# Four Strassen row pairs instead of three in the second MLP product of a fp32 encoder trunk

## The chip, the cores and the metric

The kernel runs on one core of a Trainium2 chip. The metric is the device time of one execution in microseconds. TensorE (PE) multiplies, ScalarE (ACT) and VectorE (DVE) prepare operands and take results out of PSUM, GpSimd (POOL) and SyncE (SP) issue transfers.

## The reference, cut to what matters

Two layers of an encoder with 256 tokens, a model width of 2048 and an MLP width of 8192, all in float32:

```python
for l in range(DEPTH):                       # DEPTH = 2
    ...                                      # attention, gates, x = x + merged @ w_out[l]
    h = rmsnorm(x, norm_mlp[l]) @ w_ff1[l]                 # 256x2048 @ 2048x8192
    x = x + jnp.square(jax.nn.relu(h)) @ w_ff2[l]          # 256x8192 @ 8192x2048
return rmsnorm(x, norm_final)
```

The second product, `@ w_ff2[l]`, is the one that the change touches.

## The kernel before

**Products in three passes.** Each float32 operand is split into `hi`, a cast to fp32r on ACT, and `lo`, the remainder, a subtraction on DVE. A product of two blocks is then three matmuls: hi·hi, lo·hi and hi·lo, all of them L428 in `mm` inside `gemm_s` (L415 to L486). The split of weights is in `parts` (L173): L177 is the cast on ACT that writes a `hi` tile, L178 the subtraction on DVE that writes a `lo` tile and needs that `hi`.

**Row pairs.** `gemm_s` makes 256x1024 of output from 2048 rows of weights, in eight *row pairs* of 2x128 rows, which I number 0 to 7. One transfer from SP brings a pair (`raw`, 128x2048, 1 MB). A pair is done in one of two ways:

- *plain*: eight block products, 24 matmuls of 128x512, accumulating into four PSUM banks. ACT casts and DVE subtracts 2048 columns of weights.
- *Strassen*: seven products, 21 matmuls, into seven banks. For them DVE first forms four sums of weight blocks, in the tile `sums`: L465 (1024 columns), L468 and L469 (512 each). Then the three raw blocks that are used themselves (1536 columns) and the four sums (2048 columns) each go through L177 and L178. The same sums are needed of the activations, once for each pair; `sums_of` (L359, four small operations L364 to L367) makes them when the pair is transposed in `turned_pair` (L391), which also splits them (ACT L407, DVE L408).

Inside a pair (`products`, L430) all matmuls that read `hi` tiles of weights come first, then those that read `lo`.

**Buffers.** In the MLP half there are three `hi` buffers and three `lo` buffers of 2048 columns (L175), three `raw` buffers, one `sums` buffer (L460), 52 slots for activations and eight PSUM banks, one name for all of them (`bank`). A Strassen pair uses two of the three `hi` buffers and two of the three `lo` buffers.

**Loops.** The MLP goes in four blocks of 2048 hidden columns. In each block `gemm_s` runs twice on `w_ff1` (Strassen pairs 3 and 5, table `FIRST`), then twice on `w_ff2` (table `SECOND`); in the last block the second of these is replaced by plain products (`gemm_a`). I call the two products on `w_ff2` in a block *the first half* (output columns 0 to 1023) and *the second half* (1024 to 2047). That makes seven of them in a layer and 14 in all: eight first halves and six second halves. The hidden pairs 4 to 7 are transposed while the first half runs.

**End of a product.** The eight banks are combined into four results: one copy on ACT (L477, from the bank of product 1, which only Strassen pairs use, so that it is complete after the last of them), then eight additions on DVE (L476). The next product gets its banks from there.

**Order.** Each engine's instructions stand in one fixed order. It is made when the program is built, by a scheduler with its own model of durations; at run time an engine waits at an instruction whose operands or buffers are not ready, and everything behind it on that engine waits too.

```python
FIRST, SECOND = (3, 5), (2, 4, 6)                                       # L65
hi, lo = (wpool.tile([P, 2048 if strips else 1024], F32R, tag=tag, name=tag,
                     bufs=3 if strips else hbufs)[:, :src.shape[-1]] for tag in ("hi", "lo"))
w11, w22, w21 = cut(raw[:, 512:])                                       # L470
w1, w3, w2, w4 = cut(whole_ts) if strips else cut(ts[0]) + cut(ts[1])   # L471
```

## Time and profile before

| | us |
|---|---|
| median of 3 runs | 2631.06 (2629.96 to 2631.34) |
| the profiled execution | 2630.92 |
| its span, first to last instruction | 2629.1 |
| PE busy | 2599.1 (99%) |
| DVE busy | 2116.7 (81%) |
| ACT busy | 1457.8 (55%) |
| DMA, mean rate | 194 GB/s |

Busy time is the union of an engine's instructions. A matmul of 512 columns is shown with 390 ns, but matmuls are pipelined: what one costs is read from the distance between starts. A row of the timeline merges neighbours of one kind: start, duration, engine, line, operation, output and inputs, form, count, and in brackets the idle time of the engine before it with what ended it.

### The profile page before, as it was taken

The page shows a single profiled execution, that of the slowest core. Times are in us where ns is not written, and L with a number is a line of the kernel's source. Part 1 is how long each engine was busy: PE and PEld are TensorE (multiplying, and loading weights), DVE is VectorE, ACT ScalarE, POOL GpSimd, SP SyncE. Part 2 cuts the span into 40 slices and gives each one's busy share as a digit, 9 for nine tenths or more (in the row PEclk, how much of TensorE's full clock was granted, in tenths as well). Part 3 has the DMA queues.
Part 4 walks back from the last instruction along what each step waited for, and adds up shares of the span by engine and source line. Part 5 has one row for each costly group of instructions (what it writes and reads, how often), then busy time and mean ns, then how long its engine had stood idle before and what let it go on. Part 6 is the DMA issues. An engine that isn't in the chain of part 4 may idle for free.

```text
span 2629.1 us, 32272 instructions
## 1 busy us (share of the span) xinstructions
PE 2599.1 (99%) x12498; PEld 2183.3 (83%) x12498; DVE 2116.7 (81%) x2496; ACT 1457.8 (55%) x1719; POOL 97.2 (4%) x117
## 2 busy tenths in 40 slices
PE   8999999999999999999999999999999999999998
PEld 7888888878888888888888888888788888888886
DVE  6678789789888888888667787896998888888885
ACT  6555556546655545546545555564566555455553
POOL 1100000000000010000001000000000000100000
PEclk9999999999999999999999999999999999999999
DMA  7555555555567485675565555644555765756744
GB/s 243 182 159 192 192 195 170 162 179 192 200 198 242 160 244 199 199 241 178 190 195 174 173 180 190 207 146 160 188 196 192 217 210 195 244 196 198 259 160 148
DMA packets 175258, 508.97 MB, mean 194 GB/s; under 512 B 13696, under 2 KB 18176, under 8 KB 175104
## 3 DMA queue, kind: packets, MB, share of 16 engines
q1 hardware_dynamic: 166192, 490.08, 55.7%
q0 software_dynamic: 8768, 16.78, 3.3%
q8 instruction: 98, 1.61, 0.2%
q14 instruction: 56, 0.46, 0.1%
q10 hardware_dynamic: 144, 0.04, 0.0%
HBM read 492.18 MB, written 2.10 MB: 188 GB/s over the span
## 4 chain that ended last, share of the span: by engine, by line
PE 76%; issue 19%; DVE 2%; ACT 1%; POOL 1%; DMA 0%; SPq 0%; POOLq 0%; DVEq 0%; ACTq 0%
PE bank L428 47%; PE bank L244 8%; PE bank L279 7%; PE bank L248 4%; PE bank L283 3%; PE bank L223 1%; PE bank L398 1%; DVE lo L178 1%; PE bank L252 1%; PE bank L224 1%; PE bank L254 1%; PE bank L253 1%; POOL xt L870 1%; PE bank L558 0%; ACT hi L177 0%
## 5 line engine op out<-in xcount | busy, mean ns | idle before, releaser
L428 PE MATMUL bank<-hi,pair 128*128 128x512 f32 x5156 | 1269.8, 390 | 7.0 <-ACT hi L177 6.2
L428 PEld LDWEIGHTS bank<-hi,pair 128*128 128x128 f32 x5156 | 964.9, 188 | 210.6 <-ACT hi L177 9.9
L177 ACT CAST hi<-raw 128x2048 fp32r<-128x2048 f32 (+3 forms) x416 | 630.0, 1534 | 449.1 <-PE bank L428 323.0
L178 DVE TENSOR_TENSOR lo<-raw,hi 128x2048 fp32r<-128x2048 f32 (+3 forms) x416 | 751.0, 1817 | 94.7 <-ACT hi L177 61.5
L428 PE MATMUL bank<-lo,pair 128*128 128x512 f32 x2578 | 677.4, 389 | 0.0
L428 PEld LDWEIGHTS bank<-lo,pair 128*128 128x128 f32 x2578 | 483.7, 188 | 100.2
L178 DVE TENSOR_TENSOR lo<-sums,hi 128x2048 fp32r<-128x2048 f32 (+1 forms) x134 | 254.6, 1909 | 176.3 <-ACT hi L177 118.5
L177 ACT CAST hi<-sums 128x2048 fp32r<-128x2048 f32 (+1 forms) x134 | 214.8, 1603 | 290.3 <-DVE sums L469 187.4
L202 DVE TENSOR_TENSOR lo<-raw,hi 128x1024 fp32r<-128x1024 f32 (+1 forms) x224 | 268.7, 1205 | 121.9 <-ACT hi L201 114.2
L201 ACT CAST hi<-raw 128x1024 fp32r<-128x1024 f32 (+1 forms) x224 | 230.0, 1036 | 208.6 <-PE bank L279 84.8
L244 PE MATMUL bank<-hi,pair 128*128 128x512 f32 x1024 | 259.6, 390 | 0.0
L244 PEld LDWEIGHTS bank<-hi,pair 128*128 128x128 f32 x1024 | 190.6, 188 | 38.9
L476 DVE TENSOR_TENSOR wide<-wide,bank 128x512 f32<-128x512 f32 x336 | 216.1, 680 | 4.5 <-PE bank L428 4.1
L279 PE MATMUL bank<-pair,hi 128*128 128x512 f32 x768 | 203.2, 397 | 4.5 <-ACT hi L201 3.2
L279 PEld LDWEIGHTS bank<-pair,hi 128*128 128x128 f32 x768 | 136.3, 190 | 26.9 <-ACT hi L201 3.6
L248 PE MATMUL bank<-lo,pair 128*128 128x512 f32 x512 | 142.8, 392 | 0.0
L465 DVE TENSOR_TENSOR sums<-raw 128x1024 f32<-128x1024 f32 x110 | 134.1, 1219 | 5.7 <-DMA raw<-in_w_ff 5.1
L283 PEld LDWEIGHTS bank<-pair,lo 128*128 128x128 f32 x768 | 106.9, 190 | 8.7
L283 PE MATMUL bank<-pair,lo 128*128 128x256 f32 x768 | 111.6, 283 | 0.0
L248 PEld LDWEIGHTS bank<-lo,pair 128*128 128x128 f32 x512 | 95.2, 188 | 18.9
L408 DVE TENSOR_TENSOR pair<-wide,pair 128x512 fp32r<-128x512 f32 x108 | 72.4, 686 | 13.9 <-ACT pair L407 13.9
L870 POOL DMA_DIRECT2D xt<-wide x48 | 42.3, 968 | 977.0 <-DVE wide L476 702.6
(131 smaller groups left out, 1727.8 us busy)
## 6 DMA issues: line engine op xcount, KB each, us to landing
raw<-in_w_ff SPq DMA_DIRECT2D x256, 1024.0 KB, 5.2
raw<-in_w_in SPq DMA_DIRECT2D x124, 1024.0 KB, 5.1
raw<-in_w_out SPq DMA_DIRECT2D x32, 1024.0 KB, 5.3
raw<-in_w_o_na SPq DMA_DIRECT2D x16, 1024.0 KB, 5.0
raw<-in_w_o_mla SPq DMA_DIRECT2D x16, 1024.0 KB, 5.0
xt<-wide POOLq DMA_DIRECT2D x48, 256.0 KB, 6.8
raw<-in_w_ukv SPq DMA_DIRECT2D x8, 1024.0 KB, 5.6
raw<-in_w_uq SPq DMA_DIRECT2D x8, 768.0 KB, 4.6
```

The lines of the kernel that those rows point to most:

```text
L177: nc.scalar.copy(hi, src)
L178: nc.vector.tensor_tensor(lo, src, hi.bitcast(F32), op=ALU.subtract)
L201: nc.scalar.copy(hi, src)
L202: nc.vector.tensor_tensor(lo, src, hi.bitcast(F32), op=ALU.subtract)
L244: nc.tensor.matmul(ps[t], a, wh[:, k], start=k0 + k + i == 0, stop=False)
L248: nc.tensor.matmul(ps[t], sides(have(acts, k0 + k), t)[0], wl[:, k], start=False, stop=k0 + k == nk - 1)
L279: nc.tensor.matmul(ps[m], wh[:, k, m * P:(m + 1) * P], have(acts, k0 + k), start=k0 + k == 0, stop=False)
L283: nc.tensor.matmul(ps[m][:, :S], wl[:, k, m * P:(m + 1) * P], have(acts, k0 + k)[:, :S], start=False, stop=k0 + k == nk - 1)
L408: nc.vector.tensor_tensor(lw, src, h.bitcast(F32), op=ALU.subtract)
L428: nc.tensor.matmul(b[i], x, y, start=count[i] == 1, stop=count[i] == total[i])
L465: nc.vector.tensor_tensor(ts[0].rearrange("p (a n) -> p a n", a=2), raw[:, :512].rearrange("p (a n) -> p a n", a=1).to_broadcast([P, 2, 512]),
L476: add = lambda o, a, c: nc.vector.tensor_tensor(o, a, c, op=ALU.add)
```

## The change

One table entry: the pairs that go by Strassen's algorithm in the second MLP product.

```diff
-FIRST, SECOND = (3, 5), (2, 4, 6)
+FIRST, SECOND = (3, 5), (2, 3, 5, 6)
```

In each of the 14 products on `w_ff2`, pairs 0, 1, 4 and 7 are plain now and 2, 3, 5 and 6 are Strassen. Before, a plain pair stood between any two Strassen pairs; now 2 and 3 are neighbours, and 5 and 6. Each of the eight blocks also has one more hidden pair whose sums are formed. SP's and POOL's orders are the same as before; on PE, DVE and ACT the scheduler makes another order.

**DVE, second half of a block.** Before, from the last weight sum of one Strassen pair (L469) to that of the next:

```order
L469 TENSOR_TENSOR sums<-raw,sums 128x512
L178 TENSOR_TENSOR lo<-sums,hi 128x2048
L178 TENSOR_TENSOR lo<-raw,hi 128x2048
L465 TENSOR_TENSOR sums<-raw 128x1024
L178 TENSOR_TENSOR lo<-raw,hi 128x1536
L468 TENSOR_TENSOR sums<-raw,sums 128x512
L469 TENSOR_TENSOR sums<-raw,sums 128x512
```

Now, from pair 2 to pair 3 (the first six rows) and on to pair 5:

```order
L469 TENSOR_TENSOR sums<-raw,sums 128x512
L178 TENSOR_TENSOR lo<-sums,hi 128x2048
L178 TENSOR_TENSOR lo<-raw,hi 128x1536
L465 TENSOR_TENSOR sums<-raw 128x1024
L468 TENSOR_TENSOR sums<-raw,sums 128x512
L469 TENSOR_TENSOR sums<-raw,sums 128x512
L178 TENSOR_TENSOR lo<-sums,hi 128x2048
L178 TENSOR_TENSOR lo<-raw,hi 128x2048
L465 TENSOR_TENSOR sums<-raw 128x1024
L178 TENSOR_TENSOR lo<-raw,hi 128x1536
L468 TENSOR_TENSOR sums<-raw,sums 128x512
L469 TENSOR_TENSOR sums<-raw,sums 128x512
```

Between neighbours the plain pair's subtraction (2048 columns from `raw`) is gone, and the three sums stand directly behind one another; from 3 to 5 the order is the old one. From 5 to 6 it is as from 2 to 3.

**PE, second half of a block**, from the first matmul on the sums of a Strassen pair. Before, one period (the `hi x20` rows are eight matmuls on the sums and twelve of the plain pair behind):

```order
L428 MATMUL bank<-hi,pair 128x512 x20
L428 MATMUL bank<-lo,pair 128x512 x4
L428 MATMUL bank<-hi,pair 128x512 x6
L428 MATMUL bank<-lo,pair 128x512 x8
L428 MATMUL bank<-hi,pair 128x512 x4
L428 MATMUL bank<-lo,pair 128x512 x3
L428 MATMUL bank<-hi,pair 128x512 x20
```

Now, from pair 2's sums to pair 6's (a `hi x14` row is eight on the sums of pair 2 or 5 and six on the raw blocks of pair 3 or 6; the `hi x20` rows begin with the sums of pair 3 and of pair 6):

```order
L428 MATMUL bank<-hi,pair 128x512 x14
L428 MATMUL bank<-lo,pair 128x512 x7
L428 MATMUL bank<-hi,pair 128x512 x20
L428 MATMUL bank<-lo,pair 128x512 x4
L428 MATMUL bank<-hi,pair 128x512 x6
L428 MATMUL bank<-lo,pair 128x512 x8
L428 MATMUL bank<-hi,pair 128x512 x4
L428 MATMUL bank<-lo,pair 128x512 x3
L428 MATMUL bank<-hi,pair 128x512 x14
L428 MATMUL bank<-lo,pair 128x512 x7
L428 MATMUL bank<-hi,pair 128x512 x20
```

From one Strassen pair's sums to the next there were 20+4+6+8+4+3 = 45 matmuls; now there are 14+7 = 21 between neighbours and 45 between pairs 3 and 5.

**ACT, first half of a block**, now, from the cast of pair 5's sums:

```order
L177 CAST hi<-sums 128x2048
L177 CAST hi<-raw 128x1536
L477 COPY wide<-bank 128x512
L177 CAST hi<-sums 128x2048
L177 CAST hi<-raw 128x2048 x3
```

The copy L477 that begins the end of the product now stands ahead of the cast of pair 6's sums, in all 14 products; before, it stood behind the casts of pair 7 and of the next product's pair 0.

In the first half, one product on the sums of pair 2 and one on those of pair 3 (two `hi` matmuls and one `lo` each) are also put off: on PE the matmuls of pair 4 end with `lo x8`, then come

```order
L428 MATMUL bank<-hi,pair 128x512 x8
L428 MATMUL bank<-lo,pair 128x512
L428 MATMUL bank<-hi,pair 128x512 x2
L428 MATMUL bank<-lo,pair 128x512 x4
L428 MATMUL bank<-hi,pair 128x512 x14
```

that is six on pair 5's raw blocks, then two and one on the sums of pair 2, two and one on those of pair 3, three on pair 5, and only then pair 5's sums (the first eight of `hi x14`). Until these are done, two of the three `hi` buffers are held by the sums of pairs 2 and 3.

## The prediction

> **What bounds the kernel now.** I read the waits of PE first, then the stages by window.

> ```profile
> PE 2599.1 (99%) x12498; PEld 2183.3 (83%) x12498; DVE 2116.7 (81%) x2496; ACT 1457.8 (55%) x1719; POOL 97.2 (4%) x117
> PE bank L428 <- ACT hi L177: 6.2, 6, 1.1
> core 0: us, PE busy (x) PEld busy (x) DVE busy (x) ACT busy (x) POOL busy (x), PEclk, DMA share, GB/s
> 924.10:1094.90 170.80, 170.80 (x772) 141.91 (x771) 141.56 (x128) 92.81 (x75) 7.06 (x8) 1.00 0.66 209
> 924.10:965.40 41.30, 41.30 (x184) 34.20 (x183) 34.96 (x29) 19.60 (x14) 3.52 (x4) 1.00 0.76 230
> 1046.80:1094.90 48.10, 48.10 (x222) 40.09 (x221) 40.55 (x43) 28.20 (x28) 0.00 (x0) 1.00 0.57 192
> ```

> PE is the bound. Its L428 matmuls waited for ACT's casts 6.2 us in all, six times, and never over 1.1 us. In one MLP block (170.8 us) it is never idle, while DVE is busy 141.6. Shares hide the rest, though: in the second half of a block (about 924 to 965) DVE is busy 35.0 of 41.3, and in the first half (about 1047 to 1095) 40.6 of 48.1. So I look at how DVE gets through the second half (start, duration; [idle before]):

> ```profile
> 937.57 0.68 DVE L469 TENSOR_TENSOR sums<-raw,sums 128x512 f32<-128x512 f32 x1
> 940.31 2.29 DVE L178 TENSOR_TENSOR lo<-sums,hi 128x2048 fp32r<-128x2048 f32 x1 [2.05 <-ACT hi L177]
> 942.72 2.29 DVE L178 TENSOR_TENSOR lo<-raw,hi 128x2048 fp32r<-128x2048 f32 x1
> 944.93 1.22 DVE L465 TENSOR_TENSOR sums<-raw 128x1024 f32<-128x1024 f32 x1
> 946.06 1.75 DVE L178 TENSOR_TENSOR lo<-raw,hi 128x1536 fp32r<-128x1536 f32 x1
> 947.73 0.68 DVE L468 TENSOR_TENSOR sums<-raw,sums 128x512 f32<-128x512 f32 x1
> 948.45 0.69 DVE L469 TENSOR_TENSOR sums<-raw,sums 128x512 f32<-128x512 f32 x1
> 951.20 2.29 DVE L178 TENSOR_TENSOR lo<-sums,hi 128x2048 fp32r<-128x2048 f32 x1 [2.05 <-ACT hi L177]
> 953.40 2.29 DVE L178 TENSOR_TENSOR lo<-raw,hi 128x2048 fp32r<-128x2048 f32 x1
> ...
> 959.13 0.69 DVE L469 TENSOR_TENSOR sums<-raw,sums 128x512 f32<-128x512 f32 x1
> ```

> This is a loop. After its last sum DVE stands idle 2.05 us while ACT casts the sums, and then goes round: 10.88 us from L469 to L469, then 10.68. PE needs for the same period, from the casts it waits for to the next ones:

> ```profile
> 938.37 1.91 ACT L177 CAST hi<-sums 128x2048 fp32r<-128x2048 f32 x1 [6.41 <-DVE sums L469]
> 949.25 1.91 ACT L177 CAST hi<-sums 128x2048 fp32r<-128x2048 f32 x1 [5.18 <-DVE sums L469]
> 959.93 1.91 ACT L177 CAST hi<-sums 128x2048 fp32r<-128x2048 f32 x1 [5.59 <-DVE sums L469]
> 942.56 4.70 PE L428 MATMUL bank<-hi,pair 128*128 128x512 f32 x20
> 947.10 1.07 PE L428 MATMUL bank<-lo,pair 128*128 128x512 f32 x4
> ...
> 952.76 4.70 PE L428 MATMUL bank<-hi,pair 128*128 128x512 f32 x20
> ...
> 962.96 4.70 PE L428 MATMUL bank<-hi,pair 128*128 128x512 f32 x20
> ```

> The sums are used on PE at 942.56, 952.76 and 962.96: 45 matmuls in 10.20 us, so 0.2267 us each. Their casts end at 940.28, 951.16 and 961.84 (start plus 1.91). The lead of the operands over PE is 2.3, 1.6 and 1.1 us: it shrinks by about half a microsecond each period, since 10.7 is more than 10.2. The stage is bound by PE, but the loop of DVE and ACT is as long.

> **The change part by part.** *PE, removed.* In each of 14 products one pair takes 21 matmuls for 24: 42 x 0.2267 = 9.5 us less. Transposes stay.

> *DVE and ACT, added.* Per product DVE has 1.22+0.69+0.68 (sums) + 1.75 + 2.29 - 2.29 = 4.3 us more, ACT about 1.5; per block the sums of one more hidden pair, four at 0.28 and one split of 0.69. On DVE 14 x 4.3 + 8 x 1.8 = 75 us in all, which by shares would still fit (152 of some 169 us in a block). Whether it hides is decided by the loops.

> *The loop between neighbours.* Pace on DVE, start to start, from the rows above: `lo` of the sums 2.20 (951.20 to 953.40), `lo` of 1536 columns 1.67 (946.06 to 947.73), L468 to L469 0.72, and L469 to the start of its `lo` 2.75 (948.45 to 951.20). L465 directly before L468 stands here only once:

> ```profile
> 277.97 1.23 DVE L465 TENSOR_TENSOR sums<-raw 128x1024 f32<-128x1024 f32 x1
> 279.23 0.69 DVE L468 TENSOR_TENSOR sums<-raw,sums 128x512 f32<-128x512 f32 x1
> ```

> 1.26. In the new order the loop from pair 2 to 3, and from 5 to 6, is 2.75+2.20+1.67+1.26+0.72 = 8.6 us. The cast cannot start earlier, as there is one `sums` buffer and DVE's order puts the sums behind both `lo`s. PE now has only 21 matmuls between: 4.76 us. Each such pass costs 3.84 us of lead. The pass from 3 to 5 is the old loop, 10.68 against 10.20: 0.48.

> *Second half of a block.* Lead at pair 2's sums: before, it was 2.3, having been 0.95 at the end of the first half (rows below). If the first half ends with none, 1.4 is left. PE then waits 3.84 - 1.4 = 2.4 at pair 3, 0.5 at pair 5 and 3.84 at pair 6: 6.8 us. The next stage has room to recover: the lead at a product's start rises by what DVE needs less there, as from 0.95 to 2.3 here.

> *First half.* It begins with more:

> ```profile
> 1062.00 1.91 ACT L177 CAST hi<-sums 128x2048 fp32r<-128x2048 f32 x1 [1.43 <-PE bank L428]
> 1068.24 1.92 ACT L177 CAST hi<-raw 128x2048 fp32r<-128x2048 f32 x1 [2.03 <-PE bank L428]
> 1069.86 1.98 PE L428 MATMUL bank<-hi,pair 128*128 128x512 f32 x8
> 1089.44 1.91 ACT L177 CAST hi<-sums 128x2048 fp32r<-128x2048 f32 x1 [4.53 <-DVE sums L469]
> 1092.30 4.70 PE L428 MATMUL bank<-hi,pair 128*128 128x512 f32 x20
> ```

> Pair 2's sums are cast at 1063.91 and used as the seventh matmul of the row at 1069.86, at 1071.22: a lead of 7.3, which covers the pass to pair 3. But casts here wait for PE to free a `hi` buffer ([<-PE bank L428]), and the new PE order holds two of the three buffers until two matmuls that stand behind six of pair 5. The cast of pair 5's sums can start only there, 1.91 plus about 0.15 for the signals; PE has seven matmuls meanwhile, 1.6 us: a wait of 0.5, and the lead is gone. Then comes the pass from 5 to 6, 3.84. Together 4.3; had the lead survived, 0.5; if the buffers hold up pair 3 as well, at most one pass more, 8.1. I take 4.3, since the lead of 7.3 is a row of this very place.

> *Sum.* Six second halves at 6.8 and eight first halves at 4.3 are 75 us of waits, against 9.5 saved: the profiled execution's 2630.9 becomes 2696.6. It lies 0.1 under the median of the runs, so **2696**. The loop's bounds: each of the dependent steps could run at the queue's pace (1.14 and 0.60 instead of 1.26 and 0.72, 0.24 less in 20 passes: -5 us), or the first halves could cost 8.1 (+31).

> **The rivals.** *Faster.* PE stays the bound and the three matmuls are simply gone: 2630.9 - 9.5 = 2621. It needs a lead of 7.7 us (two passes of 3.84) at pair 2 of each product. For it: 7.3 in the first half, and idle time left on DVE. Against: 2.3, 1.6, 1.1 in the second half, where PE already takes what comes.

> *First halves keep their lead* and wait 0.5 only: 2630.9 - 9.5 + 6 x 6.8 + 8 x 0.5 = 2666. For it: the lead of 7.3. Against: it falls to 0.95 already with alternating pairs.

> *The copy L477.* It now stands on ACT ahead of the cast of pair 6's sums and waits for PE's first `lo` matmul of pair 6.

> ```profile
> 965.36 0.57 ACT L477 COPY wide<-bank 128x512 f32<-128x512 f32 x1
> 965.84 1.92 ACT L177 CAST hi<-raw 128x2048 fp32r<-128x2048 f32 x1
> ```

> If DVE were in time, that alone would make PE wait: 0.39 (the matmul to its end) + 0.48 + 1.91 - 3 x 0.2267 = 2.1 us, 14 times; with the 9.5 saved that is 2651. It is hidden where the sums come later, as I expect.

> *The clock falls.* Waits of nearly 4 us are new here. Rows of the end, and of the start:

> ```profile
> 2618.00:2621.00 3.00, 0.00 (x0) 0.00 (x0) 1.13 (x4) 1.12 (x4) 0.71 (x1) 0.88 0.00 0
> 2616.23 1.07 PE L248 MATMUL bank<-lo,pair 128*128 128x512 f32 x4
> 9.37 3.54 PE L279 MATMUL bank<-pair,hi 128*128 128x512 f32 x8 [3.20 <-ACT hi L201]
> 12.75 0.49 PE L495 MATMUL bank<-ident,xt 128*128 128x128 f32 x3
> ```

> The last matmul ends at 2617.3; a mean granted clock of 0.88 over 2618 to 2621 means half clock from 2620.3, after 3.0 us of idleness. At the start eight matmuls took 3.38 us (9.37 to 12.75), 0.42 each, 1.6 us more than at full clock. If each long wait brought that, the six behind second halves and the two first halves that no second half follows would pay it in full, 8 x 1.6 = 13 us: 2709. Behind the other first halves DVE would catch up meanwhile. [...]

> **How the numbers follow.** Forecast 0.55, its own range 2686 to 2716; first halves keep their lead 0.15; clock 0.16; the copy alone 0.08; faster 0.06. The range 2655 to 2718 holds the forecast, the case at 2666 and the clock's, and leaves out the copy alone and the faster case, 0.14, and the far end of the first halves' bound. The three runs lie within 1.4 us, and I call 0.2% (5 us) the least that can be told from no change: faster 0.06, the same 0.01, slower 0.93.

> **What would show it.** L428 with 5128 and 2564 matmuls (28 and 14 fewer); PE's waits for ACT's L177 of some 75 us instead of 6.2, at four places in a block: at the sums of pair 3 and of pair 6 of the second half (2.4 and 3.8), at pair 6 of the first half (3.8), and small ones at pair 5. On DVE a period of 8.6 from L469 to L469 between neighbours, with 2 us idle each. In the `w_ff1` products no waits. The reasoning is wrong if PE's waits at pair 6 are ended by L477's place rather than by the sums, if the lead at pair 2 of the second half is well over 1.4, or if the granted clock falls below 1.00 in the blocks.

## The result, and the profile after

| | us |
|---|---|
| before, median beside it | 2630.93 |
| after, median of 4 runs | 2710.04 (2702.66 to 2716.68) |
| ratio, 95% interval | 1.0301 [1.0277, 1.0325] |
| the profiled execution, after | 2705.57, span 2703.4 |

The change makes the kernel 3.0% slower, 79 us in the medians and 74.7 in the profiled executions (2705.57 - 2630.92). The four runs spread over 14 us, where those of before spread over 1.4. First the engines' busy time of after, the largest wait of PE, and the costliest matmul groups with the idle time before them:

```profile
PE 2617.1 (97%) x12456; PEld 2184.9 (81%) x12456; DVE 2188.4 (81%) x2592; ACT 1485.4 (55%) x1741; POOL 97.3 (4%) x117
PE bank L428 <- ACT hi L177: 63.5, 36, 3.5
L428 PE MATMUL bank<-hi,pair 128*128 128x512 f32 x5128 | 1282.5, 395 | 64.1 <-ACT hi L177 63.5
L428 PE MATMUL bank<-lo,pair 128*128 128x512 f32 x2564 | 671.4, 389 | 0.0
```

The 42 matmuls are gone (12456 for 12498), and DVE has 71.7 us more to do; its share stays at 81%. PE's wait for ACT's casts is 63.5 us instead of 6.2, in 36 places, up to 3.5 us each. One surprise is in the first row: PE is *busy* 18 us longer, with fewer matmuls.

Where the waits stand shows in the timeline of PE from the end of a first half to the end of the second half behind it (start, duration; idle time before in brackets):

```profile
924.20 3.51 PE L428 MATMUL bank<-hi,pair 128*128 128x512 f32 x14 [0.41 <-ACT hi L177]
927.55 1.75 PE L428 MATMUL bank<-lo,pair 128*128 128x512 f32 x7
932.72 7.34 PE L428 MATMUL bank<-hi,pair 128*128 128x512 f32 x20 [3.42 <-ACT hi L177]
...
956.44 3.34 PE L428 MATMUL bank<-hi,pair 128*128 128x512 f32 x14
959.61 1.75 PE L428 MATMUL bank<-lo,pair 128*128 128x512 f32 x7
962.93 4.86 PE L428 MATMUL bank<-hi,pair 128*128 128x512 f32 x20 [1.57 <-ACT hi L177]
...
973.61 3.47 PE L428 MATMUL bank<-hi,pair 128*128 128x512 f32 x14 [0.16 <-ACT hi L177]
976.92 1.75 PE L428 MATMUL bank<-lo,pair 128*128 128x512 f32 x7
982.18 4.14 PE L428 MATMUL bank<-hi,pair 128*128 128x512 f32 x10 [3.52 <-ACT hi L177]
```

The first three rows are pairs 5 and 6 of a first half, the rest pairs 2, 3, 5 and 6 of the second half. DVE in the same second half, from the last weight sum of one Strassen pair (L469) to that of the next:

```profile
951.17 0.69 DVE L469 TENSOR_TENSOR sums<-raw,sums 128x512 f32<-128x512 f32 x1
954.32 2.29 DVE L178 TENSOR_TENSOR lo<-sums,hi 128x2048 fp32r<-128x2048 f32 x1 [2.46 <-ACT hi L177]
...
960.18 0.69 DVE L469 TENSOR_TENSOR sums<-raw,sums 128x512 f32<-128x512 f32 x1
962.91 2.29 DVE L178 TENSOR_TENSOR lo<-sums,hi 128x2048 fp32r<-128x2048 f32 x1 [2.04 <-ACT hi L177]
...
970.85 0.69 DVE L469 TENSOR_TENSOR sums<-raw,sums 128x512 f32<-128x512 f32 x1
973.59 2.29 DVE L178 TENSOR_TENSOR lo<-sums,hi 128x2048 fp32r<-128x2048 f32 x1 [2.05 <-ACT hi L177]
...
979.45 0.69 DVE L469 TENSOR_TENSOR sums<-raw,sums 128x512 f32<-128x512 f32 x1
```

From pair 5 to 6 the loop takes 979.45 - 970.85 = 8.60 us, from 3 to 5 it takes 10.67, each with 2 us of idleness while ACT casts the sums. PE has 21 matmuls, 4.76 us, for the short one.

The larger part of the surprise is explained by the windows: each row below is one stretch of 3.41 us, with the time that PE is busy, and behind the five engines the granted clock. These stretches are laid on the grid on which the clock changed in this execution.

```profile
927.86:931.27 3.41, 1.44 (x7) 0.86 (x5) 2.80 (x4) 1.09 (x2) 0.00 (x0) 1.00 0.00 0
931.27:934.69 3.42, 1.97 (x5) 1.60 (x6) 1.99 (x1) 3.42 (x3) 0.00 (x0) 0.50 0.77 222
934.69:938.10 3.41, 3.41 (x10) 2.67 (x9) 3.41 (x3) 3.14 (x2) 0.00 (x0) 0.50 0.21 85
938.10:941.51 3.41, 3.41 (x17) 2.80 (x16) 2.03 (x3) 0.34 (x1) 0.00 (x0) 1.00 0.94 265
...
2122.52:2125.93 3.41, 1.79 (x8) 1.42 (x8) 1.81 (x1) 3.41 (x3) 0.00 (x0) 1.00 0.76 211
2125.93:2129.34 3.41, 3.41 (x17) 2.82 (x16) 3.41 (x3) 1.35 (x1) 0.00 (x0) 1.00 0.24 96
...
2303.43:2306.84 3.41, 1.20 (x6) 0.70 (x5) 1.33 (x3) 2.47 (x2) 0.00 (x0) 1.00 0.43 70
2306.84:2310.25 3.41, 3.41 (x9) 2.64 (x9) 3.41 (x2) 2.61 (x2) 0.00 (x0) 0.50 0.62 247
```

Behind some waits (927.86, 2303.43) the clock is at half for one or two stretches: 9 or 10 matmuls in 3.41 us instead of 16 or 17. Behind others (2122.52) it stays at 1.00. It fell nine times in this execution, for 41 us in all, before the fall at its end (2695.96). Adding up, over all matmuls at half clock, what each took beyond 226.6 ns gives 16.7 us.

From the starts of the matmuls of 512 columns I made the same ledger for every kernel below: *waits* is the time between two starts beyond 226.6 ns at full clock, less the 9.4 us that before has by this count; *half clock* is the sum just described; *saved* is matmuls by 0.2267. For after: -9.5 + 65.5 + 16.7 = 72.7 of the 74.7 measured. By this count the waits, less what is saved, are some three quarters of the loss, and the clock is most of the rest. (The two are not independent, as the run with the products of zeros shows below.)

### The profile page after: what moved, and what is told of

Same layout as the page of the kernel before. It is cut to its first block, busy times and chain, and to the rows that moved or that the text cites. A ratio compares the mean times of both kernels' runs of the same rounds, so it can differ in the third digit from the quotient of the medians.

```text
span 2703.4 us, 32294 instructions
## 1 busy us (share of the span) xinstructions
PE 2617.1 (97%) x12456; PEld 2184.9 (81%) x12456; DVE 2188.4 (81%) x2592; ACT 1485.4 (55%) x1741; POOL 97.3 (4%) x117
## 4 chain that ended last, share of the span: by engine, by line
PE 68%; issue 21%; DVE 6%; ACT 3%; DMA 1%; POOL 0%; SPq 0%; DVEq 0%; POOLq 0%; ACTq 0%
PE bank L428 41%; PE bank L244 8%; PE bank L279 6%; PE bank L248 4%; PE bank L283 3%; DVE lo L178 3%; ACT hi L177 2%; PE bank L223 1%; DVE sums L465 1%; PE bank L398 1%; PE bank L252 1%; PE bank L224 1%; PE bank L254 1%; PE bank L253 1%; DVE sums L469 1%
## 5 line engine op out<-in xcount | busy, mean ns | idle before, releaser
L428 PE MATMUL bank<-hi,pair 128*128 128x512 f32 x5128 | 1282.5, 395 | 64.1 <-ACT hi L177 63.5
L428 PEld LDWEIGHTS bank<-hi,pair 128*128 128x128 f32 x5128 | 968.6, 190 | 284.5 <-ACT hi L177 80.9
L177 ACT CAST hi<-raw 128x2048 fp32r<-128x2048 f32 (+3 forms) x416 | 624.2, 1521 | 479.4 <-PE bank L428 337.9
L178 DVE TENSOR_TENSOR lo<-raw,hi 128x2048 fp32r<-128x2048 f32 (+3 forms) x416 | 743.5, 1800 | 101.5 <-ACT hi L177 58.8
L428 PE MATMUL bank<-lo,pair 128*128 128x512 f32 x2564 | 671.4, 389 | 0.0
L428 PEld LDWEIGHTS bank<-lo,pair 128*128 128x128 f32 x2564 | 481.0, 188 | 99.8
L178 DVE TENSOR_TENSOR lo<-sums,hi 128x2048 fp32r<-128x2048 f32 (+1 forms) x148 | 286.7, 1945 | 165.1 <-ACT hi L177 129.3
L177 ACT CAST hi<-sums 128x2048 fp32r<-128x2048 f32 (+1 forms) x148 | 241.6, 1632 | 247.0 <-DVE sums L469 135.5
L201 ACT CAST hi<-raw 128x1024 fp32r<-128x1024 f32 (+1 forms) x224 | 230.5, 1038 | 203.0 <-PE bank L279 85.2
L279 PE MATMUL bank<-pair,hi 128*128 128x512 f32 x768 | 203.4, 397 | 3.8 <-ACT hi L201 2.5
L465 DVE TENSOR_TENSOR sums<-raw 128x1024 f32<-128x1024 f32 x124 | 151.3, 1220 | 9.1 <-DMA raw<-in_w_ff 7.9
L279 PEld LDWEIGHTS bank<-pair,hi 128*128 128x128 f32 x768 | 136.3, 190 | 26.3 <-ACT hi L201 2.9
L248 PE MATMUL bank<-lo,pair 128*128 128x512 f32 x512 | 141.8, 392 | 0.0
L248 PEld LDWEIGHTS bank<-lo,pair 128*128 128x128 f32 x512 | 95.3, 188 | 19.1
L408 DVE TENSOR_TENSOR pair<-wide,pair 128x512 fp32r<-128x512 f32 x116 | 78.0, 687 | 11.6 <-ACT pair L407 11.5
L469 DVE TENSOR_TENSOR sums<-raw,sums 128x512 f32<-128x512 f32 x124 | 85.2, 687 | 1.3
```

Of the source, the lines that this page charges most:

```text
L177: nc.scalar.copy(hi, src)
L178: nc.vector.tensor_tensor(lo, src, hi.bitcast(F32), op=ALU.subtract)
L201: nc.scalar.copy(hi, src)
L248: nc.tensor.matmul(ps[t], sides(have(acts, k0 + k), t)[0], wl[:, k], start=False, stop=k0 + k == nk - 1)
L279: nc.tensor.matmul(ps[m], wh[:, k, m * P:(m + 1) * P], have(acts, k0 + k), start=k0 + k == 0, stop=False)
L428: nc.tensor.matmul(b[i], x, y, start=count[i] == 1, stop=count[i] == total[i])
```

## The experiments

My theory by then: the loop of the sums between neighbouring Strassen pairs makes the waits (one `sums` buffer; DVE stands idle while ACT casts), and the clock falls behind some of them. The rivals were that DVE simply has too much to do in a product, that the cast's duration is what counts, and that the clock is the main cause.

**The sums in two halves.** If DVE's idle 2 us are the price, half a cast would halve it. The split alone, on the old pairs, is its control.

```diff
+            if strips:
+                sh, sl = (wpool.tile([P, 2048], F32R, tag=tag, name=tag, bufs=3) for tag in ("hi", "lo"))
+                nc.scalar.copy(sh[:, :1024], ts[0])
 ...
+                nc.scalar.copy(sh[:, 1024:], ts[1])
+                for h in range(2):
+                    hs = slice(h * 1024, (h + 1) * 1024)
+                    nc.vector.tensor_tensor(sl[:, hs], ts[h], sh[:, hs].bitcast(F32), op=ALU.subtract)
```

> The changed kernel (pairs 2, 3, 5, 6), but the cast of the weight sums on ScalarE is made in two halves: the first behind L465, while VectorE still makes the other two sums, the second behind L469; the subtraction in two halves too. This takes the idle 2.05 us out of VectorE's loop; matmuls and VectorE's elements stay the same. Theory (waits come from the loop sum, cast, subtraction): the loop between neighbours goes from 8.6 to about 1.26+0.72+0.60+1.67+2x1.14 = 6.5 us against 4.76 on TensorE, so a pass costs 1.8 us of lead for 3.84; TensorE's waits for casts of sums fall from about 65 us to under 15, no clock falls, 2621 to 2635 us. Rival (VectorE simply has too much work, 75 us more): time stays at 2690 to 2715. Rival (buffers or the copy L477): waits at pair 6 stay above 2 us, 14 times, 2650 or more.

> The kernel before (pairs 2, 4, 6) with the same cast in two halves. It is the control: TensorE waits 6 us in all there, so theory and rivals expect 2629 to 2632 us, no change, with a longer lead at the sums in the second half than 2.3, 1.6 and 1.1 us. If splitting helps or hurts by itself, it shows here.

The split kernel took 2722.82 us, ratio 1.0349 [1.0334, 1.0365], slower still; the control 2642.21, 1.0043 [1.0029, 1.0058]. My expectation of the first was wrong, and so was that of the control (2629 to 2632). The largest waits of PE in the first:

```profile
PE bank L428 <- ACT hi L470: 36.9, 26, 1.9
PE bank L428 <- ACT hi L177: 16.6, 53, 1.1
```

The long waits became many short ones, none over 1.9 us; together they come to some 95 us by the ledger. The loop on DVE only shrank from 8.6 to 7.9 (976.47 to 984.34 between last sums), because after them DVE now waits 1.1 us for the cast of the raw blocks, which on ACT now stands behind the first half-cast:

```profile
976.47 0.69 DVE L472 TENSOR_TENSOR sums<-raw,sums 128x512 f32<-128x512 f32 x1
978.29 1.76 DVE L178 TENSOR_TENSOR lo<-raw,hi 128x1536 fp32r<-128x1536 f32 x1 [1.12 <-ACT hi L177]
```

The control shows that the split costs 11 us by itself. So this pair of runs doesn't isolate the cast. The runs below go at the loop in other ways.

**Same pairs, other places.** The row order in a product is changed, so that plain and Strassen pairs alternate: the work is that of the change, nothing is left out, but no Strassen pairs are neighbours.

```diff
-                gemm_s(w2, g * 1024, lambda j: have(hid, j), range(8), SECOND, residual2)
+                gemm_s(w2, g * 1024, lambda j: have(hid, j), (0, 2, 1, 3, 4, 5, 7, 6), SECOND, residual2)
```

> The changed kernel with the same four Strassen pairs, but taken in the order 0, 2, 1, 3, 4, 5, 7, 6, so that a plain pair stands between any two. Matmuls and VectorE's work as in the changed kernel. If only neighbourhood costs (every pass 10.68 against 10.20), about 0.5 us per pass and the 9.5 us are kept: 2622 to 2632 us. If the sum of a product counts (VectorE with its idle time at the casts: 4 x 6.3 + 4 x 2.2 + 8 x 0.6 + three times 2.1 = 45 us against 40.7 on TensorE), some 4.5 us of waits per second half and 1 to 2 per first half remain: 2650 to 2670 us. In both cases the waits are shorter than 3 us and the granted clock falls less often.

**Old amount, one pair of neighbours.** Three Strassen pairs as before the change, but two of them neighbours:

```diff
-FIRST, SECOND = (3, 5), (2, 3, 5, 6)
+FIRST, SECOND = (3, 5), (2, 3, 6)
```

> Three Strassen pairs as before, but 2, 3 and 6: two neighbours, no more work than before. If neighbourhood costs: at pair 3 of each second half 3.84 less a lead of 2.3, that is a wait of 1.5 us, six times, the first halves covered by their lead of 7.3: about 2640 us. If only the sum of a product counts (40.7 us on VectorE against 41.4 on TensorE, as before): 2631 us.

Alternating gave 2654.84 us, 1.0091 [1.0074, 1.0108]; neighbours with the old amount 2637.14, 1.0024 [1.0014, 1.0034]. The second has six new waits of 0.92 us, all at pair 3 of second halves, though a product has no more to do than before; they are shorter than the 1.5 I had worked out. The first loses 24 us to before with no neighbours at all: its waits add 28.8 and the half clock 4.4, with 9.5 saved. They are waits of another kind. For casts PE waits 6.9 us in all, hardly more than the 6.2 of before; the largest sum is

```profile
PE bank L428 <- DVE lo L178: 9.5, 10, 1.5
```

with six waits of 1.45 us where a first half passes into a second one, for a subtraction of raw blocks. Another six, of 0.57, stand for the copy L477 behind second halves, and the rest is small. In this row order the last pair of a product is a Strassen pair, so its end has changed as well, and the run is no clean test of neighbourhood. What it shows is that the same pairs cost 55 us less (2710.04 - 2654.84) where none are neighbours, and that PE then no longer waits for casts of sums.

**Two buffers for the sums.** The prediction says that the sums of the next pair can't start before both subtractions of this one, since there is one `sums` buffer. A second one takes that away, and the order on DVE can change with it. (The space comes from the scratch memory for transfers.) The control is the kernel before with the same two lines.

```diff
-                whole_ts = spool.tile([P, 2048], F32, tag="sums", name="sums", bufs=1)
+                whole_ts = spool.tile([P, 2048], F32, tag="sums", name="sums", bufs=2)
-    ... dynamic_dma_scratch_size=8192)
+    ... dynamic_dma_scratch_size=4096)
```

> The changed kernel (pairs 2, 3, 5, 6) with two buffers for the weight sums instead of one (4 KB for it are taken from the ring of POOL's transfers). VectorE can now form the sums of the next Strassen pair while ScalarE casts those of this one; in the new order pair 3's first sums stand ahead of pair 2's subtractions, and pair 6's ahead of pair 5's. Work and matmuls are the same. Theory (the loop sum, cast, subtraction, closed by the single buffer): the idle 2 us at each cast go, a second half needs about 39 to 41 us on VectorE against 40.7 on TensorE; TensorE's waits for casts of sums fall from 65 us to under 15, the clock does not fall, 2621 to 2635 us. Rival (VectorE's 75 us more work do not fit, whatever the order): 2690 or more. Rival (hi and lo buffers, or the copy L477): waits of 2 us or more stay at pair 6, 2650 to 2670 us.

> The kernel before (pairs 2, 4, 6) with two buffers for the sums and the same smaller ring: the control. TensorE waits hardly at all there, so nothing is to be had: 2629 to 2632 us by all theories. If the smaller ring costs something, it shows here.

With the change: 2646.02 us, 1.0059 [1.0046, 1.0071]. On the old pairs: 2632.63, 1.0005 [0.9996, 1.0015], no difference. The very same work as in the change, and 64 of its 79 us are gone: the single buffer, with the order on DVE that it forces, was the cause of most of it, and not the amount of work. My 2621 to 2635 was too good, though. DVE and PE of this kernel, at the end of the same second half, and its wait for the weights' transfers in the whole execution:

```profile
944.86 2.29 DVE L178 TENSOR_TENSOR lo<-sums,hi 128x2048 fp32r<-128x2048 f32 x1 [1.45 <-ACT hi L177]
950.28 1.23 DVE L465 TENSOR_TENSOR sums<-raw 128x1024 f32<-128x1024 f32 x1 [1.46 <-DMA raw<-in_w_ff]
...
960.55 0.69 DVE L469 TENSOR_TENSOR sums<-raw,sums 128x512 f32<-128x512 f32 x1
961.96 2.29 DVE L178 TENSOR_TENSOR lo<-sums,hi 128x2048 fp32r<-128x2048 f32 x1 [0.71 <-ACT hi L177]
961.98 4.37 PE L428 MATMUL bank<-hi,pair 128*128 128x512 f32 x11 [1.83 <-ACT hi L177]
DVE sums L465 <- DMA raw<-in_w_ff: 32.9, 34, 2.2
```

Pair 2's and pair 3's sums are now made ahead of both pairs' subtractions of sums, and PE no longer waits at pair 3. What is late next is a transfer: at 950.28 DVE is ready for pair 5's sums, and the weights aren't there (32.9 us in 34 places in the whole execution, against 7.9 in 7 places in after). PE's wait has moved with it: the row at 961.98 begins with the sums of pair 5, 66 matmuls behind those of pair 2, and pair 6's sums are then there in time. Each second half still pays 1.5 to 2.5 us at pair 5, each first half 0.6 there. The ledger: -9.5 + 17.9 + 2.8 = 11.2 of 13.8 (2644.73 - 2630.92). That the transfer makes the wait at pair 5 is a reading of the rows: from 950.28 to the last sum DVE is never idle, and the 1.46 us would cover most of the 1.83. A fourth `raw` buffer would test it; I did not run one.

**Two buffers and alternating order.** Both remedies at once:

> Two buffers for the sums and the same four Strassen pairs in the order 0, 2, 1, 3, 4, 5, 7, 6. If the loop with its idle time at the cast is all that cost something in the alternating order as well (there 38 us of waits for 9.5 us saved), it goes: 2621 to 2635 us, no clock falls. If other waits were part of it (results taken out of PSUM by VectorE late in a product, seen as waits for L178 and L477 there), some 10 us of them stay: 2635 to 2645 us.

This was not what I expected: 2664.32 us, 1.0126 [1.0112, 1.014], worse than either alone. Its largest waits of PE, and DVE's for transfers:

```profile
PE bank L428 <- ACT wide L477: 12.0, 12, 1.6
PE bank L428 <- ACT hi L177: 10.0, 13, 2.0
PE bank L428 <- DVE lo L178: 9.0, 9, 2.0
DVE sums L465 <- DMA raw<-in_w_ff: 52.1, 40, 3.0
```

Here the wait for transfers is larger still, and the banks at the end of a product (L477) come late. Which of these makes the other I can't tell from this run; it stays open why the two remedies don't add.

**The waits without the clock.** Two products of zeros, added into a bank that is being summed, stand on PE ahead of the sums at pair 6 and, in second halves, at pair 3. They change no result and break up the idle time, while the operands are as late as before.

```diff
+    zero = const.tile([P, P], F32, name="zero")
+    nc.gpsimd.memset(zero, 0.0)
 ...
+            if pairs == SECOND and (j == 6 or j == 3 and c0 == 1024):
+                for _ in range(2):
+                    nc.tensor.matmul(b[5], zero, t1, start=False, stop=False)
```

> The changed kernel, with two more float32 matmuls of a zero block with the first weight sums, added to the bank of product 5 (they add zero), ahead of the sums' matmuls of pair 6 in all products and of pair 3 in second halves, where TensorE waits anyway. They break its idle stretches of 3.6 and 2.4 us into pieces of under 2 us. Theory of the clock (the falls cost 12 to 17 us beside the waits): no falls or few in the MLP blocks, the loop's waits remain, 2688 to 2698 us, and less scatter between runs than the 14 us of the changed kernel. Rival (the half clock is hidden behind the loop, since VectorE catches up meanwhile): 2703 to 2717 us as before. If the two matmuls take more than the wait, some us more in either case.

2691.99 us (2691.4 to 2692.96), 1.0233 [1.0219, 1.0247]. PE's place at pair 6 of the same first half, where each product of zeros shows as two matmuls, and the stretch of all MLP blocks:

```profile
927.08 1.98 PE L477 MATMUL bank<-sums,zero 128*128 128x512 f32 x4
930.46 4.83 PE L430 MATMUL bank<-hi,pair 128*128 128x512 f32 x20 [1.40 <-ACT hi L179]
740.00:2660.00 1920.00, 1891.43 (x8785) 1554.57 (x8784) 1581.35 (x1740) 1050.66 (x1114) 69.31 (x80) 1.00 0.59 192
```

No fall is left: the `hi x20` behind the wait takes 4.83 us, not 7.34. The time is 18 us below that of the change, and the runs spread over 1.6 us instead of 14. So the clock accounts for about 18 us in the medians, 14 in the profiled executions (2705.57 - 2691.66), and for nearly all of the scatter. The ledger: -9.5 + 52.5, and the 80 matmuls of the zeros, which fill what were waits, 80 x 0.2267 = 18.1, are 61.1 of 60.7 (2691.66 - 2630.92). The loop's waits are all still there, and 5 us more of them, 52.5 + 18.1 = 70.6 against 65.5: without a fall every second half loses 2.2 to 2.4 us at pair 3 and 3.6 to 3.7 at pair 6, while in after five of the six lose less at one of the two, each time behind a fall (1.73 us at pair 3, or some 2.55 at pair 6). While PE runs at half clock, the sums catch up. In the prediction's terms the loop is the cause and the clock an addition.

**First halves alone.** Four pairs in the first halves as in the change; in the second halves three, alternating with plain ones, as before.

```diff
-                gemm_s(w2, g * 1024, lambda j: have(hid, j), range(8), SECOND, residual2)
+                gemm_s(w2, g * 1024, lambda j: have(hid, j), (0, 1, 2, 4, 3, 5, 6, 7) if g else range(8),
+                       (2, 3, 6) if g else SECOND, residual2)
```

> Four pairs (2, 3, 5, 6) in the eight first halves as in the change; in the six second halves three pairs (2, 3, 6) in the row order 0, 1, 2, 4, 3, 5, 6, 7, so that a plain pair stands between any two of them, as before the change. 24 matmuls are saved: 2630.9 - 5.4 = 2625.5 without waits. Theory that each half of a block loses what its own loop loses (3.6 + 0.6 in a first half, 2.2 in the two first halves of the two blocks that open a layer): 2625.5 + 6 x 4.2 + 2 x 2.2 = 2655, and up to 10 us more if the clock falls behind each long wait: 2652 to 2666. Rival, that the second halves of the change leave the next stages without a lead and the first halves pay for that: each first half costs what the opening ones did or less, 2625.5 + 8 x 2.2 = 2643 or less.

> The same with two buffers for the weight sums. With them the trace of the full change has in a first half only the wait of 0.6 + 0.1 at pair 5, for a hi buffer that two products put off hold. If the single buffer is the whole cause of the pass from 5 to 6 here too: 2625.5 + 8 x 0.7 = 2631, within 2628 to 2634, no change against the kernel before. If the casts or the transfers of the weights hold the sums up instead, 2640 or more.

With one buffer 2674.56 us, 1.0161 [1.0145, 1.0177]; with two 2633.74, 1.0011 [1.0002, 1.002]. In the first, six first halves wait 0.58 and 3.6 us, the two that open a layer 2.18, just as in the full change: what a first half loses does not come from the second half ahead of it. The waits are 31.0 us, where 6 x 4.2 + 2 x 2.2 = 29.6 were expected; the total is 9 us beyond my range because the clock fell behind every one of the six long waits, for two stretches each (17.1 us, I had allowed 10). The ledger: -5.4 + 31.0 + 17.1 = 42.7 of 43.1 (2674.0 - 2630.9). One fall, in the windows of this kernel:

```profile
922.07:925.48 3.41, 0.79 (x4) 0.33 (x2) 2.18 (x3) 1.72 (x2) 0.00 (x0) 1.00 0.03 6
925.48:928.89 3.41, 2.59 (x6) 2.11 (x7) 2.61 (x2) 3.41 (x3) 0.00 (x0) 0.50 0.95 287
928.89:932.31 3.42, 3.42 (x9) 2.65 (x9) 3.42 (x2) 2.87 (x2) 0.00 (x0) 0.50 0.33 38
932.31:935.72 3.41, 3.41 (x16) 2.81 (x16) 1.74 (x3) 0.00 (x0) 0.00 (x0) 1.00 0.80 306
```

With two buffers the waits of 3.6 and 2.2 are gone, and 0.6 at pair 5 remains: for a first half the single buffer was the whole cause of the pass from 5 to 6. But the 5.4 us saved are eaten up (the waits add 5.3, one fall ahead of the second layer's MLP blocks 1.6), so this is no gain either. No version that I ran beats the kernel before.

## Why the prediction was right, and where not

2696 us was predicted, 2655 to 2718; 2710 is inside, and inside the likeliest case's own range (2686 to 2716).

- **PE, removed**: 42 matmuls by 0.2267, as counted.
- **The loop between neighbours**: 8.6 from L469 to L469 was predicted, 8.60 measured; 3.84 lost per pass, 3.6 to 3.7 measured. The two-buffer run confirms the reason that was given (one `sums` buffer, DVE's order); it changes the two together.
- **The pass from 3 to 5**: 0.48 predicted, 0.3 measured.
- **Second half**: 2.4 + 0.5 + 3.84 = 6.8 predicted. Where the clock held until pair 6, 2.35 + 0.3 + 3.67 = 6.3 (the one with pair 3 at 2124). Where it had fallen in the first half just before, pair 3 waited less: 1.73 from start to start, the row at 962.93 (whose 1.57 in brackets is the idle time alone). Where it fell behind pair 3, pair 6 waited 2.55 only. With no falls, in the run with products of zeros, all six lose 2.2 to 2.4 and 3.6 to 3.7. The lead of 1.4 at pair 2 was therefore right.
- **First half**: 0.5 + 3.84 = 4.3 predicted; 0.57 + 3.6 = 4.2 measured in six of eight. (The 0.15 for the signals: in rows of before DVE is idle 2.05 us for a cast of 1.91, 0.14 more.) The two that open a layer waited 2.18 only. The term was put for all eight from rows of a later block. Rows of after say what differs (two of an opening first half, then one of a later):

```profile
741.35 1.91 ACT L177 CAST hi<-sums 128x2048 fp32r<-128x2048 f32 x1
742.94 3.34 PE L428 MATMUL bank<-hi,pair 128*128 128x512 f32 x14
...
922.24 1.91 ACT L177 CAST hi<-sums 128x2048 fp32r<-128x2048 f32 x1 [0.53 <-PE bank L428]
```

  In the opening one the cast of pair 5's sums follows the one ahead of it without a wait and ends at 743.26. PE's row begins with six matmuls on raw blocks, so the sums are used at 744.30: a lead of 1.0 us survives into the pass to 6, as I read it. PE's order differs there too, with 24 matmuls between the two pairs' sums for 21, another 0.7. Of the 3.84 that leaves 2.1.
- **Sum of the waits**: 75 predicted, 65.5 measured, and 70.6 in the run with products of zeros, where no fall shortens them. Most of the 5 that are left are the two opening first halves, 2 x 2.1. That run, the loop without the clock, took 2692, 4 below the forecast.
- **The copy L477** was dismissed, rightly: at pair 6 the cast of the sums is still held by DVE's last sum when the copy is over.

```profile
928.88 0.59 ACT L477 COPY wide<-bank 128x512 f32<-128x512 f32 x1 [3.35 <-PE bank L428]
930.76 1.90 ACT L177 CAST hi<-sums 128x2048 fp32r<-128x2048 f32 x1 [1.29 <-DVE sums L469]
```

- **The clock** is the step that was wrong. The forecast had it at 1.00 in the blocks and named its fall as what would refute the reasoning; it fell, as in the rival at 2709, whose 13 us measured as 16.7, or as 14 when the waits that it shortens are taken off (2705.57 - 2691.66). The rival was right in size but not in its manner, by which each of eight long waits pays 1.6. Of nine waits of about 3.6 us six brought a fall, of nine of 2.2 to 2.6 three did, and a fall cost 1.9 us on average here (16.7 over nine) and 2.9 in the first-halves kernel (17.1 over six). Ahead of the result no run showed a wait of nearly 4 us amid matmuls; that the clock would hold behind it, on which 2696 rests, was my estimate. In this trace every fall starts at a multiple of 3.413 us from the others and, but for the one that ends the execution, lasts one or two of these; and the stretch ahead of the fall was not always idle throughout: the one at 927.86 has 1.44 us of work in its 3.41.

So the total came nearer than its parts, by two errors of opposite sign: 10 us too much for the waits (5 of them because the falls shorten the waits) and 17 too little for the clock. That they nearly cancel is luck.

## What to carry to other kernels

Work that is added to a helper engine is judged by the dependent chain around one buffer (here sums, cast, subtraction, sums again), in the shortest interval in which the bounding engine asks for two of them; DVE's share, 81% before and after, showed nothing of it. If such a chain must be run twice in a row, a second buffer for its first link is the first thing to try: here it took back 64 of 79 us. And a wait in a dense stream of matmuls can cost more than its length: in after, of nine waits of 2.2 to 2.6 us three were followed by half clock, and of nine of about 3.6 six, at 1.9 us a fall on average.

## What the runs showed of the hardware

```profile
2272.71:2276.12 3.41, 1.83 (x9) 1.18 (x7) 3.22 (x4) 0.67 (x2) 0.00 (x0) 1.00 0.00 0
2276.12:2279.54 3.42, 1.55 (x7) 1.30 (x8) 1.57 (x1) 3.42 (x2) 0.00 (x0) 1.00 0.66 180
2279.54:2282.95 3.41, 3.41 (x17) 2.77 (x16) 3.41 (x3) 3.37 (x3) 0.00 (x0) 1.00 0.31 127
```

So a wait of 2.4 us brought it (2303.43) while one of 3.6 that the grid cuts in two did not. But this border is not a rule for other kernels. In the one with the four pairs alternating, this stretch with 0.46 idle was followed by half clock:

```profile
759.35:762.76 3.41, 1.85 (x7) 0.99 (x7) 3.41 (x5) 0.00 (x0) 0.00 (x0) 1.00 0.91 285
762.76:766.17 3.41, 3.41 (x10) 2.62 (x9) 3.38 (x7) 1.29 (x1) 1.38 (x2) 0.50 0.38 43
```

In after one with 0.46 idle was not (750.36, 1.85 us busy of 3.41, as here). PE's busy time, whose ends are modelled, is thus not all that decides, and what else does stays open. The clock came back in after at the end of the first stretch in which PE was idle for at most 0.11 of it (2143.01, 3.03 us busy); stretches with 0.40 to 0.42 kept it low (931.27, 1.97 busy), and in the first-halves kernel one with 0.24 (925.48, 2.59 busy). So the falls in the blocks lasted one or two stretches.
